# Placing the second half's gate operands and squares behind the gate's sigmoids

## The chip, the cores and the metric

One Trainium2 chip, one core of it. The metric is the device time of one execution in microseconds (us); of several executions the median is given. Engines are named as in the profile: PE is TensorE's matmul, PEld its weight load, DVE VectorE, ACT ScalarE, POOL GpSimd, SP SyncE (which issues most DMAs).

## What is computed

One layer of a decoder trunk for 1024 prompt positions and 8 single new tokens (1032 columns in all), model width 1024. After the mixing part and the squared-ReLU MLP, the layer ends with the step that matters here, and a final normalisation follows:

```
x = x + (p @ w_ple) * sigmoid(rms_norm(x, g_ple) @ w_ple_gate)     # p: (tokens, 256)
y = rms_norm(x, g_final)
```

Activations are kept transposed: the model width lies on partitions (8 blocks `m` of 128) and tokens lie along the free axis.

## The kernel before, in words

Each fp32 product is made of three fp32r products. An operand is split into a high part (`hi`, a cast on ACT) and a rest (`lo`, on DVE), and PE adds hi·hi, lo·hi and hi·lo.

**The two halves.** The down-projection of the MLP (`down`, L1434) and all that follows treat the tokens as two halves `nn` = 0, 1 of 516 columns. x lies in `ACC[:, ab, nn, p]` (L1309), where `m = p + 4*ab`. Half 0 is complete before the down stage ends, half 1 with its last steps.

**What the gate needs of x.** For each of the eight blocks (ab, p) of a half:
- `gate_in` (L1425) makes the matmul operands `XS[ab, nn]`: one ACT activation that scales by the gain `g_ple` (recorded as L166), and one DVE operation for the rest (L167). For half 1 these tiles are called `xt`, for half 0 `xs`.
- `add_ss` (L1389) adds the block's squares into `ss[:, nn]`: the first block by one ACT Square (L1398), each later one by an ACT Square into the only `sq` buffer (L1394) and a POOL add (L1395). It does so at high priority (`PRI`).

Then `rows_tok` (L1402) sums over partitions on PE (ten one-column matmuls into `ms`, L1408), takes the inverse root on DVE and puts it on diagonals in `sq`; `rows_all` (L1417) spreads it over all partitions (PE, `rB`, L1422) and two ACT copies (L1423) bring it back to `ss[:, nn]`, now the row factor `rr`. For half 0 `rows_all` is called in the last step of the down stage, so its two copies are the last readers of two of the down stage's eight PSUM banks.

**The gate stage.** From L1516 on, PSUM is four banks for gate sums (`psg2`, tile `g`) and four for all else (`pss2`, tag `s2`: the transposes `pT` of the embedding, the embedding products `em`, later the output's transposes `yT`). `gate_units` (L1639) walks over m and over two column blocks `n` of a half: 24 matmuls a unit (L1658 to L1660), then `evg` (L1642): DVE multiplies by `rr` (L1645), ACT takes the sigmoid (L1646), PE makes `em` (L1601 to L1603), DVE multiplies the two (L1647), POOL adds to x (L1649). The first sixteen units are half 0 (blocks 0 and 2), the other sixteen half 1 (blocks 1 and 3). The weights of a block m are cast two m ahead (`whi` on ACT, L150; `wlo` on DVE, L153). At the stage's start `w_ple` is loaded and split too (`wpl`, L1555 to L1559).

**The order.** On PE it is the order in which the code is traced, written out by hand: `weave` runs the gate units, each of which yields its cost in planned us, and wakes helpers at their due times (`spawn` and `wake`): `p_in` (L1566) makes the embedding's transposes, one every 0.5 planned us, ACT casting each (`pp`, L1582) and DVE taking the rest (L1583); `second_half` (L1680) issues one (ab, p) block of half 1 every 2.0 planned us from 6.0 on, and 4.0 after the last of these steps calls `rows(1)`; `first_out` makes the output of half 0. A gate result whose `rr` or embedding is not there yet is held back and evacuated when it `arrived` (L1671). On ACT, DVE and POOL the program's builder sets the order, from priorities and from its own estimate of when operands are ready; an engine then runs its instructions in that order. `tc.issue_after(ins)` places the instructions traced inside it behind `ins` on the engine of `ins`. `placed` (L1221) is a dictionary that the up stage already uses for such instructions.

Of the kernel before, what the change touches and what calls it, by code (L numbers as in the profile page):

```python
# [12 lines left out]
AF = mybir.ActivationFunctionType  # L13
ALU = mybir.AluOpType
# [13 lines left out]
PRI = 1000  # L28
# [56 lines left out]
def trunk_step_kernel(  # L85
# [35 lines left out]
    V, S, G, PE, SY = nc.vector, nc.scalar, nc.gpsimd, nc.tensor, nc.sync  # L121
# [23 lines left out]
    def f32(ap):  # L145
        return ap.bitcast(F32)
# [18 lines left out]
    def split_gain(dst, src, gain):  # L165
        S.activation(dst[0], src, AF.Copy, scale=gain)  # L166
        V.scalar_tensor_tensor(dst[1], in0=src, scalar=gain, in1=f32(dst[0]), op0=ALU.mult, op1=ALU.subtract)  # L167
# [52 lines left out]
    def spawn(gen, delay=0.0):  # L220
        tasks.append([clock[0] + delay, gen])
# [9 lines left out]
    def weave(main):  # L231


        for cost in main:
            clock[0] += cost
            wake()

    def drain(until=lambda: False):
        while tasks and not until():
            clock[0] = max(clock[0], min(t[0] for t in tasks))  # L240
            wake()
# [43 lines left out]
    with ExitStack() as mix:  # L285
# [46 lines left out]
        gmix, gff, gple, gfin = (vec[:, 8 * i : 8 * i + 8] for i in range(4))  # L332
# [21 lines left out]
        for n, (o, w) in enumerate(BLK):  # L354
# [20 lines left out]
            for k in range(KD):  # L375
# [6 lines left out]
                else:  # L382
# [3 lines left out]
                                       op0=ALU.mult, op1=ALU.mult)  # L386
# [834 lines left out]
    placed = {}  # L1221
# [87 lines left out]
    ACC = pacc.tile([P, 2, 2, 4, 516], F32, name="acc")  # L1309
# [13 lines left out]
    XS = {(ab, 0): [xst.tile([P, 4, 516], F32R, name=f"xs{ab}{i}") for i in range(2)] for ab in range(2)}  # L1323
# [62 lines left out]

    begun = set()

    def add_ss(ab, nn, p):  # L1389

        a = ACC[:, ab, nn, p]
        with tc.high_priority(PRI):
            if nn in begun:
                S.activation(sq, a, AF.Square)  # L1394
                G.tensor_add(ss[:, nn], ss[:, nn], sq)  # L1395
            else:
                begun.add(nn)
                S.activation(ss[:, nn], a, AF.Square)  # L1398
# [26 lines left out]
    def gate_in(ab, nn, p):  # L1425
        m = p + 4 * ab
        hi, lo = XS[ab, nn]
        split_gain((hi[:, p], lo[:, p]), ACC[:, ab, nn, p], gple[:, m : m + 1])
# [119 lines left out]
    def next_w():  # L1548

        halves()  # L1550
        stage()
        cur[0] += 1
        return ready[cur[0] - 1]
# [12 lines left out]
    def p_in():  # L1566

        for nn in range(2):
            for q0 in (0, 2, 4):
                qs = (q0, q0 + 1) if q0 < 4 else (4,)  # L1570
                if 4 in qs:
                    G.tensor_scalar_mul(pt8[nn], pt8[nn], mst[: TS // 2, nn, 4:5])
                for k in range(2):
                    ps = pss.tile([P, 512], F32, tag="s2", name="pT")
                    w = 0
                    for q in qs:
                        src = pt[:, pcol(nn, q), :] if q < 4 else pt8[nn]
                        r = rows_of(q)
                        PE.transpose(ps[:, w : w + r], src[:, k * P : (k + 1) * P], ident[:r, :r])
                        w += r  # L1580
                    hi, lo = (h[:, nn, q0 * P : q0 * P + w] for h in pp[k])
                    S.copy(hi, ps[:, :w])  # L1582
                    V.tensor_sub(lo, ps[:, :w], f32(hi))  # L1583
                    yield PT
            arrived("p", nn)

    def blk(v, n):

        return v[:, n % 2, TOFF[n // 2] : TOFF[n // 2] + WT[n // 2]]

    def x_of(m, n):
        return ACC[:, m // 4, n % 2, m % 4, TOFF[n // 2] : TOFF[n // 2] + WT[n // 2]]

    def emb(m, n):

        c = slice(m * P, m * P + P)
        ps = pss.tile([P, 512], F32, tag="s2", name="em")[:, : WT[n // 2]]
        for k in range(2):
            wh, wl = wpl[k]
            xh, xl = (blk(h, n) for h in pp[k])  # L1600
            PE.matmul(ps, lhsT=wh[:, c], rhs=xh, start=(k == 0), stop=False)  # L1601
            PE.matmul(ps, lhsT=wl[:, c], rhs=xh, start=False, stop=False)
            PE.matmul(ps, lhsT=wh[:, c], rhs=xl, start=False, stop=(k == 1))  # L1603
        return ps
# [5 lines left out]
    def rows(nn):  # L1610
        rows_tok(pss.tile([P, 512], F32, tag="s2", name="ms"), nn)
        yield 8.0
        rows_all(lambda: pss.tile([P, 512], F32, tag="s2", name="rB"), nn)
        arrived("r", nn)

    def y_out(nn, q):

        r = rows_of(q)
        c = pcol(nn, q)
        yo = ty.tile([P, D], F32, tag="yo", bufs=2, name="yo")  # L1620
        st = tp.tile([P, 2], F32, tag="st2", bufs=2, name="st2")
        pa = []
        for a in range(2):
            ps = pss.tile([P, 512], F32, tag="s2", name="yT")
            for j in range(4):
                PE.transpose(ps[:r, j * P : j * P + P], ACC[:, a, nn, j, q * P : q * P + r], ident)
            S.activation(yo[:r, :512], ps[:r], AF.Square, accum_out=st[:r, a : a + 1])
            pa.append(ps)
            yield YT
        V.tensor_add(st[:r, 0:1], st[:r, 0:1], st[:r, 1:2])  # L1630
        V.scalar_tensor_tensor(st[:r, 0:1], in0=st[:r, 0:1], scalar=1.0 / D, in1=ems[:r, nn, q : q + 1], op0=ALU.mult, op1=ALU.add)
        root(st[:r, 0:1], "ry", nn == 1)
        y = y_prompt[0, c * P : (c + 1) * P, :] if q < 4 else y_sample[4 * nn : 4 * nn + 4, 0, :]
        for a in range(2):
            b = slice(512 * a, 512 * a + 512)
            V.scalar_tensor_tensor(yo[:r, b], in0=pa[a][:r], scalar=st[:r, 0:1], in1=gfb[:r, b], op0=ALU.mult, op1=ALU.mult)
            SY.dma_start(y[:, b], yo[:r, b])

    def gate_units(blocks, last):  # L1639
        for m in range(KD):  # L1640

            def evg(ps, n, m=m):  # L1642
                w = WT[n // 2]
                t = tp.tile([P, 260], F32, tag="t", name="t")[:, :w]
                V.tensor_mul(t, ps, blk(rr, n))  # L1645
                S.activation(t, t, AF.Sigmoid)  # L1646
                V.tensor_mul(t, t, emb(m, n))  # L1647
                xv = x_of(m, n)
                (V if last and m > 5 else G).tensor_add(xv, xv, t)  # L1649

            ws = next_w()
            for n in blocks:
                w = WT[n // 2]
                ps = gps[0].tile([P, 512], F32, tag="g", name="g")[:, :w]
                for k in (4, 5, 6, 7, 0, 1, 2, 3):
                    wh, wl = (h[:, k % 4, :] for h in ws[k // 4])
                    xh, xl = (h[:, k % 4, TOFF[n // 2] : TOFF[n // 2] + w] for h in XS[k // 4, n % 2])
                    PE.matmul(ps, lhsT=wh, rhs=xh, start=(k == 4), stop=False)  # L1658
                    PE.matmul(ps, lhsT=wl, rhs=xh, start=False, stop=False)  # L1659
                    PE.matmul(ps, lhsT=wh, rhs=xl, start=False, stop=(k == 3))  # L1660
                    if k == 3:
                        with tc.high_priority(PRI):
                            if there >= {("p", n % 2), ("r", n % 2)}:
                                evg(ps, n)
                            else:
                                held.append((n, lambda ps=ps, n=n, evg=evg: evg(ps, n)))
                    yield 3 * w * 0.000455
# [12 lines left out]
    def second_half():  # L1680

        for p in range(4):
            for ab in (1, 0):
                gate_in(ab, 1, p)
                add_ss(ab, 1, p)
                yield 2.0
        yield 4.0
        yield from rows(1)

    def first_out():  # L1690
        for q in range(5):
            yield from y_out(0, q)

    with tc.manual_schedule(engines={mybir.EngineType.PE}):
        spawn(p_in())
        spawn(second_half(), 6.0)
        weave(gate_units((0, 2), False))
        spawn(first_out(), FIN0)
        weave(gate_units((1, 3), True))
        drain()  # L1700
        for q in range(5):
            for _ in y_out(1, q):
                pass
# [32 lines left out]
```

## Time and profile before

| | us |
|---|---|
| median of 3 runs (1418.0 to 1418.56) | 1418.04 |
| the profiled execution, its own time | 1419.37 |
| span of the profile, first to last instruction | 1417.7 |

Mean granted TensorE clock 0.965 of full speed. The end of the span is laid out like this: the down stage's last matmuls until 1254 us, the gate stage until 1396 us (half 1's units from 1327 us), and the output of half 1 until 1417.7 us. Busy time of an engine is shown with its share; an idle time in a row names what ended it in square brackets, behind an arrow.

### The profile page before, as it was taken

To read this page: it belongs to the slowest core of one execution; us is meant where nothing else is said; L and a number is where in the kernel's file an instruction comes from. 1 tells how busy PE (TensorE), PEld (TensorE's weight loads), DVE (VectorE), ACT (ScalarE), POOL (GpSimd) and SP (SyncE) were. 2 spreads that over 40 slices of the span, in tenths; PEclk is the share of its full clock that TensorE was granted. 3 is DMA by queue.
4 is the path that set the end of the run, shared out by engine and by line. 5 is a ranking of instruction groups with operands and counts; after the bars stand their busy time and mean duration, and the time that the engine had idled before them with its cause. 6 is when DMAs were issued, how large, how long until landed. Compare 5 with 4: busy or idle time off the path is not lost.

```text
span 1417.7 us, 26668 instructions
## 1 busy us (share of the span) xinstructions
PE 1314.5 (93%) x10189; PEld 1280.7 (90%) x10189; DVE 913.8 (64%) x1900; ACT 638.3 (45%) x1346; POOL 693.4 (49%) x720
## 2 busy tenths in 40 slices
PE   6979978999999799899999999789999999979995
PEld 5979968889899799899999999789999998979985
DVE  7745745465937757655544445677878787975564
ACT  6574645532233316556544555333433333552332
POOL 5300888857414405578848777731425156532110
PEclk9999988999999999999999999899999999999997
DMA  7234535555436721254446554873363523122221
GB/s 244 90 90 118 151 81 151 173 158 153 136 86 180 229 71 44 60 164 145 141 143 194 154 178 143 312 264 125 122 222 112 200 93 91 61 89 76 80 86 61
DMA packets 212076, 194.01 MB, mean 137 GB/s; under 512 B 20952, under 2 KB 181659, under 8 KB 211940
## 3 DMA queue, kind: packets, MB, share of 16 engines
q1 hardware_dynamic: 211436, 190.45, 43.5%
q8 instruction: 80, 1.31, 0.4%
q0 software_dynamic: 512, 1.85, 0.3%
q14 instruction: 48, 0.39, 0.1%
HBM read 131.75 MB, written 60.61 MB: 136 GB/s over the span
## 4 chain that ended last, share of the span: by engine, by line
PE 66%; DVE 11%; POOL 9%; ACT 4%; DMA 3%; issue 3%; SPq 0%; DVEq 0%; POOLq 0%; ACTq 0%
PE A L1184 9%; PE D L1184 6%; PE d L1457 6%; PE d L1458 6%; PE d L1456 6%; PE g L209 5%; PE g L211 5%; PE g L210 4%; PE C L1184 3%; PE B L1184 3%; POOL xinv L644 3%; POOL it L643 3%; DVE wlo L153 2%; PE g L1658 2%; PE g L1659 2%
## 5 line engine op out<-in xcount | busy, mean ns | idle before, releaser
L209 PE MATMUL g<-ra,whi 128*128 128x384 f32 (+3 forms) x800 | 273.2, 341 | 0.8 <-ACT ra L388 0.6
L1457 PE MATMUL d<-h,wlo 128*128 128x260 f32 (+1 forms) x896 | 256.9, 287 | 14.3 <-DVE wlo L153 14.3
L1456 PE MATMUL d<-h,whi 128*128 128x260 f32 (+1 forms) x896 | 254.6, 284 | 3.9 <-ACT whi L150 3.9
L211 PE MATMUL g<-ra,whi 128*128 128x384 f32 (+3 forms) x800 | 257.0, 321 | 0.8 <-POOL ra L389 0.4
L1458 PE MATMUL d<-h,whi 128*128 128x260 f32 (+1 forms) x896 | 256.1, 286 | 0.0
L210 PE MATMUL g<-ra,wlo 128*128 128x384 f32 (+3 forms) x800 | 255.9, 320 | 0.0
L1457 PEld LDWEIGHTS d<-h,wlo 128*128 128x128 f32 x896 | 171.4, 191 | 16.7 <-DVE wlo L153 16.7
L1456 PEld LDWEIGHTS d<-h,whi 128*128 128x128 f32 x896 | 172.1, 192 | 4.7 <-ACT whi L150 4.6
L1458 PEld LDWEIGHTS d<-h,whi 128*128 128x128 f32 x896 | 171.9, 192 | 0.0
L209 PEld LDWEIGHTS g<-ra,whi 128*128 128x128 f32 x800 | 154.9, 194 | 3.0 <-ACT ra L388 1.0
L211 PEld LDWEIGHTS g<-ra,whi 128*128 128x128 f32 x800 | 154.0, 193 | 2.5 <-POOL ra L389 1.6
L210 PEld LDWEIGHTS g<-ra,wlo 128*128 128x128 f32 x800 | 155.0, 194 | 0.7 <-DVE wlo L153 0.3
L153 DVE TENSOR_TENSOR wlo<-s,whi 128x512 fp32r<-128x512 f32 x96 | 73.7, 769 | 79.9 <-ACT whi L150 79.5
L153 DVE TENSOR_TENSOR wlo<-st,whi 128x512 fp32r<-128x512 f32 x94 | 72.3, 769 | 47.5 <-ACT whi L150 47.0
L1184 PE MATMUL A<-fb,whi 128*128 128x260 f32 (+1 forms) x512 | 95.6, 281 | 0.0
L643 POOL TENSOR_TENSOR it<-ainv,xinv 32x31 f32<-32x31 f32 (+15 forms) x124 | 74.5, 601 | 39.1 <-DMA ainv<-inv_d 29.7
L150 ACT CAST whi<-s 128x512 fp32r<-128x512 f32 x96 | 59.3, 618 | 73.8 <-PE D L1184 27.3
L1347 ACT CAST h<-raw 128x1024 fp32r<-128x1024 f32 (+1 forms) x56 | 58.7, 1055 | 68.3 <-DMA raw<-f_d 40.4
L150 ACT CAST whi<-st 128x512 fp32r<-128x512 f32 x96 | 59.0, 619 | 67.1 <-PE g L211 32.4
L1348 DVE TENSOR_TENSOR h<-raw,h 128x1024 fp32r<-128x1024 f32 (+1 forms) x56 | 76.8, 1380 | 14.6 <-ACT h L1347 14.5
L1465 DVE TENSOR_TENSOR acc<-acc,d 128x256 f32<-128x256 f32 (+1 forms) x192 | 75.0, 415 | 17.0 <-PE d L1458 16.1
L1214 ACT ACTIVATE q<-q 128x512 f32<-128x512 f32 (+1 forms) x124 | 75.9, 631 | 22.0 <-DVE q L1207 16.1
(433 smaller groups left out, 3532.2 us busy)
## 6 DMA issues: line engine op xcount, KB each, us to landing
a<-in_w_down SPq DMA_DIRECT2D x16, 1024.0 KB
raw<-f_d SPq DMA_DIRECT2D x28, 520.0 KB
raw<-f_d SPq DMA_DIRECT2D x28, 512.0 KB
st<-in_w_in SPq DMA_DIRECT2D x24, 512.0 KB
ck<-ck_d SPq DMA_DIRECT2D x32, 320.0 KB
ra<-in_w_up SPq DMA_DIRECT2D x32, 256.0 KB
rb<-in_w_up SPq DMA_DIRECT2D x32, 256.0 KB
st<-in_w_ple_gate SPq DMA_DIRECT2D x16, 512.0 KB
```

What stands on the lines that cost most here:

```text
L150: S.copy(dst_hi, src)
L153: lo_eng.tensor_sub(dst_lo, src, f32(dst_hi))
L209: PE.matmul(ps[:, :w], lhsT=whi[k], rhs=xh, start=(k == 0), stop=False)
L210: PE.matmul(ps[:, :w], lhsT=wlo[k], rhs=xh, start=False, stop=False)
L211: PE.matmul(ps[:, :w], lhsT=whi[k], rhs=xl, start=False, stop=(k == nk - 1))
L643: G.tensor_mul(tv, a, x)
L1184: PE.matmul(ps, lhsT=a[:, k, :], rhs=x[:, c, k, :], start=(first and k == 0 and j == 0), stop=(k == 3 and j == 2), skip_group_check=True)
L1214: placed["act"] = S.activation(v, v, func).ins
L1348: V.tensor_sub(lo[:, c], raw[:, c], f32(hi[:, c]))
L1456: PE.matmul(ps, lhsT=wh[:, k, :], rhs=xh[:, k, :], start=(k == 0), stop=False)
L1457: PE.matmul(ps, lhsT=wl[:, k, :], rhs=xh[:, k, :], start=False, stop=False)
L1458: PE.matmul(ps, lhsT=wh[:, k, :], rhs=xl[:, k, :], start=False, stop=(k == 3))
```

## The change

A sigmoid of the gate is remembered each time one is traced. `second_half` starts at 7.0 planned us and issues a block every 2.8. In it the ACT half of `gate_in` and the Square of `add_ss` are placed behind the latest sigmoid traced so far, the DVE half is written out beside them unplaced, and these squares have no raised priority. The step after the last block is 3.0.

```
-    def add_ss(ab, nn, p):
+    def add_ss(ab, nn, p, first=True):
         a = ACC[:, ab, nn, p]
-        with tc.high_priority(PRI):
+        with tc.high_priority(PRI if first else 0):
...
-                S.activation(t, t, AF.Sigmoid)
+                placed["sig"] = S.activation(t, t, AF.Sigmoid).ins
...
         for p in range(4):
             for ab in (1, 0):
-                gate_in(ab, 1, p)
-                add_ss(ab, 1, p)
-                yield 2.0
-        yield 4.0
+                m = p + 4 * ab
+                (hi, lo), x = XS[ab, 1], ACC[:, ab, 1, p]
+                with tc.issue_after(placed["sig"]):
+                    S.activation(hi[:, p], x, AF.Copy, scale=gple[:, m : m + 1])
+                V.scalar_tensor_tensor(lo[:, p], in0=x, scalar=gple[:, m : m + 1], in1=f32(hi[:, p]), op0=ALU.mult, op1=ALU.subtract)
+                with tc.issue_after(placed["sig"]):
+                    add_ss(ab, 1, p, False)
+                yield 2.8
+        yield 3.0
         yield from rows(1)
...
-        spawn(second_half(), 6.0)
+        spawn(second_half(), 7.0)
```

## Rows read from the trace of the kernel before

**Rows 1.** The profile's page, part 1: busy time, share of the span and instructions of each engine.
```profile
PE 1314.5 (93%) x10189; PEld 1280.7 (90%) x10189; DVE 913.8 (64%) x1900; ACT 638.3 (45%) x1346; POOL 693.4 (49%) x720
```

**Rows 2.** The view of waits, PE alone, from 1250 us to the end: who waited, for what, us in total, times, longest.
```profile
PE yT L1626 <- DVE yo L1636: 7.6, 4, 4.2
PE pT L1579 <- ACT ss L1423: 7.1, 1, 7.1
PE em L1601 <- DVE yo L1636: 2.4, 1, 2.4
PE pT L1579 <- DVE t L1647: 1.2, 1, 1.2
```

**Rows 3.** The chain that ended last, in order of time, from 1247 to 1280 us: start us, us, what.
```profile
1248.78 7.61 DMA st<-in_w_ple
1256.40 1.04 ACT wpl L150
```

**Rows 4.** The timeline of ACT: start us, us, line, operation, tiles, shapes, count.
```profile
1257.36 3.19 ACT L166 ACTIVATE xt<-acc,vec 128x516 fp32r<-128x516 f32 x5
1260.44 0.35 ACT L1423 COPY ss<-rB 128x256 f32<-128x256 f32 x1
1260.70 1.96 ACT L166 ACTIVATE xt<-acc,vec 128x516 fp32r<-128x516 f32 x3
1262.55 0.36 ACT L1423 COPY ss<-rB 128x260 f32<-128x260 f32 x1
...
1265.21 0.63 ACT L1394 ACTIVATE sq<-acc 128x516 f32<-128x516 f32 x1 [1.15 <-POOL ss L1395]
...
1270.26 1.28 ACT L1646 ACT_TABLE_LOAD   x1
1271.55 0.42 ACT L1646 ACTIVATE t<-t 128x256 f32<-128x256 f32 x1
...
1272.46 0.61 ACT L150 CAST whi<-st 128x512 fp32r<-128x512 f32 x1
...
1279.19 0.42 ACT L1646 ACTIVATE t<-t 128x256 f32<-128x256 f32 x1 [0.85 <-DVE t L1645]
...
1286.38 0.42 ACT L1646 ACTIVATE t<-t 128x256 f32<-128x256 f32 x1 [3.12 <-DVE t L1645]
```

**Rows 5.** The timeline of PE around the start of the gate stage, with the two steps of `rows(1)` at its end.
```profile
1253.49 1.03 PE L1422 MATMUL rB<-sq,ones 128*128 128x256 f32 x4
...
1255.54 0.28 PE L1660 MATMUL g<-xs,whi 128*128 128x256 f32 x1
1262.97 0.69 PE L1579 MATMUL pT<-ident,pt 128*128 128x128 f32 x2 [7.14 <-ACT ss L1423]
...
1266.17 0.38 PE L1579 MATMUL pT<-ident,pt 128*128 128x128 f32 x2
...
1267.11 0.38 PE L1579 MATMUL pT<-ident,pt 128*128 128x128 f32 x2
...
1270.17 0.28 PE L1601 MATMUL em<-pp,wpl 128*128 128x256 f32 x1
...
1273.35 0.28 PE L1660 MATMUL g<-xs,whi 128*128 128x256 f32 x1
1274.85 0.44 PE L1579 MATMUL pT<-ident,pt 128*128 128x128 f32 x2 [1.22 <-DVE t L1647]
...
1302.78 1.07 PE L1408 MATMUL ms<-ones,ss 128*128 128x1 f32 x10
...
1314.22 1.03 PE L1422 MATMUL rB<-sq,ones 128*128 128x256 f32 x4
```

**Rows 6.** Half-microsecond stretches of PE: from:to, length, busy us (instructions), granted clock (1.00 is 2.4 GHz, 0.50 is 1.2 GHz), DMA share, GB/s.
```profile
1259.00:1259.50 0.50, 0.00 (x0) 0.50 0.12 35
...
1265.50:1266.00 0.50, 0.50 (x5) 0.68 0.00 0
...
1361.50:1362.00 0.50, 0.50 (x4) 0.50 0.99 361
...
1364.50:1365.00 0.50, 0.50 (x5) 0.69 0.00 0
```

**Rows 7.** The timeline of PE after a shorter wait, in half 1; the second and the third row are the first and the last of 16 matmuls in a row.
```profile
1360.44 0.36 PE L1601 MATMUL em<-pp,wpl 128*128 128x256 f32 x1 [2.35 <-DVE yo L1636]
...
1361.49 0.42 PE L1660 MATMUL g<-xt,whi 128*128 128x260 f32 x1
...
1364.74 0.32 PE L1660 MATMUL g<-xt,whi 128*128 128x260 f32 x1
```

**Rows 8.** The timeline of DVE at the start of the gate stage.
```profile
1258.62 5.42 DVE L167 SCALAR_TENSOR_TENSOR xt<-acc,vec,xt 128x516 fp32r<-128x516 f32 x8
...
1273.10 1.37 DVE L153 TENSOR_TENSOR wlo<-st,whi 128x512 fp32r<-128x512 f32 x1 [0.88 <-ACT whi L150]
1274.39 0.41 DVE L1647 TENSOR_TENSOR t<-t,em 128x256 f32<-128x256 f32 x1
...
1281.53 0.69 DVE L153 TENSOR_TENSOR wlo<-st,whi 128x512 fp32r<-128x512 f32 x1 [1.46 <-ACT whi L150]
```

**Rows 9.** The timeline of POOL at the same place.
```profile
1272.63 1.28 POOL L1395 TENSOR_TENSOR ss<-ss,sq 128x516 f32<-128x516 f32 x1 [1.34 <-ACT sq L1394]
```

**Rows 10.** Busy time in one long stretch of half 0's units: from:to, length, PE, PEld, DVE, ACT, POOL (instructions), clock, DMA share, GB/s.
```profile
1276.50:1336.00 59.50, 59.50 (x497) 59.04 (x496) 28.69 (x71) 18.38 (x40) 13.43 (x18) 1.00 0.25 72
```

## The prediction

> **What bounds the kernel now.** I read the page's part 1 first: PE is busy for 93% of the span [rows 1], so other engines' work costs time only where PE stands still or runs at the lower clock. Next comes the view of waits for PE, from the start of the gate stage on [rows 2]: of its 18.3 us, 10.0 belong to the output stage (yT and em behind yo), which the change does not touch; 7.1 are one single wait for the copy `ss` (L1423), 1.2 another for `t` (L1647). These two lie where the change is made.
>
> The chain says what came before the copy [rows 3]: the DMA of `w_ple` lands at 1256.40, and ACT casts it until 1257.44. The ACT timeline shows the rest [rows 4]: five of half 1's `xt` activations run ahead of the first copy and three more ahead of the second, which ends at 1262.91. The factors `rB` that are copied were finished by PE at 1254.52 [rows 5]. PE's first transpose `pT` needs the PSUM bank that the second copy gives back, so PE stands from 1255.82 to 1262.97. Nobody needs `xt` before half 1's units, some 65 us later; ACT runs them because their operands are there. After the wait PE runs at 1.2 GHz: the granted clock is 0.50 from 1259.0 and rises at about 1265.7 [rows 6]. Two groups of two transposes and six matmuls took 1263.0 to 1266.17, 3.20 us, and the next group at full clock 0.94 [rows 5], so the clock costs 3.20 - 1.88 = 1.32 us.
>
> The second wait (1.22 us at 1274.85) [rows 5]: a `pT` needs the `s2` bank that held the first `em`; that is free when DVE has done t·em, 1274.39 to 1274.80, and this stood behind a `wlo` of 1.37 us [rows 8], whose cast ran at 1272.46 behind a Square that came late [rows 4].
>
> From 1276.5 to 1336.0 PE is never idle [rows 10], so what is won before that is carried through half 0.
>
> **The change, part by part.**
>
> *The eight `xt` activations leave the place ahead of the copies.* They are now behind a sigmoid, and the first sigmoid needs transposes that wait for the copies; so no `xt` can be ahead of them. The copies then follow the last `wpl` cast: first at about 1257.36 (where the first `xt` started), second 0.26 us later, the pitch from a copy to the next instruction [rows 4], ending at 1257.62 + 0.36 = 1257.98. PE resumes 0.06 us later as before, at 1258.04 instead of 1262.97: **-4.93 us**. Bounds: not less, unless other ACT work takes the place (a rival); at most 2.2 more, the remaining wait from 1255.82, if the copies also got ahead of the `wpl` casts. I take the low end: the builder had five `xt` between `wpl` and the copies, so by its own estimate the copies were ready later than the casts, and nothing in the change makes them ready sooner.
>
> *The clock.* A wait of 2.2 us remains. The trace has one of 2.35 us at 1360.44; behind it the clock fell too, and 16 matmuls from 1361.49 to 1364.74 came 0.217 us apart [rows 6, 7], against 59.50/497 = 0.120 [rows 10]: 15 × 0.097 = 1.45 us. The ends are 0 (clock kept, gain 1.32) and 1.45. I take 1.45, the nearest wait in length: **+0.13 us**.
>
> *The squares leave the embedding's casts alone.* Before, each Square waited about 1.15 us for the POOL add that frees `sq` [rows 4], with the `pp` casts queued behind it on ACT. Now the first sigmoid comes right behind the casts and its table load (1.28 us), and t·em of the first unit can run once `em` is done, before the `pT` that waited. If DVE keeps its order, with `wlo` ahead, t·em waits for the weights' cast, which PE releases at the end of the second unit, 1272.4 before and so no later relative to PE; with `wlo` at 0.69 instead of 1.37 [rows 8] and its cast not behind a Square (0.1), the wait shrinks from 1.22 to about 0.45. Ends: 0 and 1.22; I take the unchanged order: **-0.8 us**.
>
> *What the gate stage takes on.* ACT gets eight times 0.72 + 0.64 us, DVE eight L167 (5.42 us in all) [rows 8], POOL eight adds of 1.28 [rows 9]. A block falls due every 2.8 planned us. Two sigmoids of the same column block, two units apart, stand 7.19 us apart [rows 4], against 24 × 516 × 0.000455 = 5.63 planned: one planned us is 1.28 real, so a block comes about every 3.6 us, one a unit. Per unit ACT then holds 0.42 + 0.62 + 1.36 = 2.4 of 3.6 us, and DVE and POOL were busy for 48% and 23% of the stretch [rows 10]. Queued behind a placed pair are the next sigmoid and weight cast. A sigmoid late by 1.4 us holds one of four gate banks longer, a cast is needed two units after its buffer is free: nothing on PE, **0**. Without that cover (the pressed banks of the first three units) it could cost up to one pair, 1.36.
>
> *`rows(1)` moves* from 6.0 + 16.0 + 4.0 = 26.0 to 7.0 + 22.4 + 3.0 = 32.4 planned us, its spread from 34.0 to 40.4; each wake is rounded up to the next gate step, some 2 us more in all. Half 1's first unit begins at 8 × 5.63 = 45.1, so the spread is still ahead of it. DVE has 8 planned us, here 1314.22 - 1302.78 = 11.4 real [rows 5], as before. The eighth block starts at the earliest 5.8 planned (7.4 real) us ahead of the sums, and takes about 4.2: gate multiply and sigmoid 0.85, `xt` 0.72, Square 0.64, perhaps an x add 0.74, its own add 1.28. Slack 3.2 us: **0**. The first Square, issued early in the down stage, goes with them; ACT waited there anyway: 0. No DMA is added or moved; the gate weights' loads follow PE's releases and come earlier with them.
>
> **Sum:** -4.93 + 0.13 - 0.8 = -5.6 us. The profiled execution took 1419.37 (its span 1417.7 and 1.67 around it), 1.33 above the median; it would come to 1413.8, the median to 1418.04 - 5.6 = **1412.4 us**.
>
> **The rivals.**
>
> 1. *All of the wait goes.* The copies run at 1254.6, the clock stays, the second wait goes: 2.2 + 4.93 + 1.32 + 1.22 = 9.7, so 1408.4. Against it: the order just argued. Chance 0.12.
> 2. *Collisions in the first units.* A `wlo` that ran beside an add of squares took 1.37 us, one with POOL idle 0.69 [rows 8, 9]. The adds, once bunched in 16 us, are now spread over eight units, and each holds DVE up to its 1.28 us. On PE's path is only what the `s2` banks wait for while `p_in` still runs: two such, 2.6 us, leaving 3.0: 1415.0. Against: DVE is idle half the time, and the first placed pair comes after the second sigmoid. Chance 0.12. The Trainium skill has the rule ("SBUF — State Buffer", Who interferes with whom): a VectorE instruction with two SBUF inputs and a GpSimd one that reads SBUF share a read port, and the second waits until the first has finished. By that rule, the trace's 1.37 us agrees, and it speaks against spreading the adds.
> 3. *It doesn't do it.* Other work takes the place of `xt` ahead of the copies, or what PE wins is lost at the output stage, whose order the builder also sets anew: 1417 to 1419. For it: 10.0 us of PE's waits stand there. Against: they are DVE's own chain, which shifts with PE. Chance 0.11.
> 4. *Slower.* The blocks slip: one `sq` buffer ties each Square to the add before it, and POOL runs that add behind an x add that waits for t·em. If each block slips 1.5 us past its unit, the eighth is 12 late; PE stands at the sums for what goes beyond the 3.2 slack, 8.8 us: +3.2, so 1421.2. It decides from 3.2 us of slip in all, and is slower than before from 8.8. Against: 2.4 of 3.6 us on ACT. Chance 0.07.
>
> **How the numbers follow.** The forecast has 0.58; its own range, from a clock that stays and no second wait (-7.5) to no gain from the second wait (-4.8), is 1410.5 to 1413.2. The range reaches to rivals 1 and 2: 1408.3 to 1415.2, leaving out rivals 3 and 4. A measurement of this kernel tells about 0.2%, 2.8 us, from no change: forecast and rivals 1 and 2 are faster (0.82), rival 3 the same (0.11), rival 4 slower (0.07).
>
> **What would show it.** On ACT the two copies stand right behind the `wpl` casts and all `xt` behind sigmoids, one a unit; PE's wait for L1423 is 2.2 us, its clock falls once, the wait for L1647 is under 0.5 us, and no wait stands at L1408 or L1422. I am wrong if the copies are still late, if PE waits for `ss` of half 1 or for `pp`, or if the second half of the stage grows by what the first loses.

## The result, and the profile after

The changed kernel takes 1412.03 us (median of 19 runs, 1407.09 to 1418.24), the kernel before 1418.32 beside it (19 runs, 1415.17 to 1424.89). The two medians are 6.3 us apart; the ratio on record, which is not that of the medians, is 0.9946, interval 0.9935 to 0.9957: 7.7 us less (6.1 to 9.2). The forecast was 1412.4, 5.6 us less than before.

The profiled execution of the changed kernel is its longest: 1418.24 us. It reached the gate stage 9.2 us later than the profiled execution of before did, by differences ahead of the changed code (the same kernel reached it at 1253.49 in e8, below), so the two spans (1416.5 and 1417.7) are not compared. What is compared is one stretch, called the stage from here on: from the start of its first rB matmul (L1422) to the start of the first output transpose yT (L1626). Before, it lasts from 1253.49 [rows 5] to 1333.6, 80.1 us; after, from 1262.70 to 1334.0, 71.3 us. The second profile of the changed kernel, e8, gives 72.0. So the stage is shorter by 8.1 to 8.8 us, which the interval of the whole runs holds.

The page of the changed kernel, part 1, answers to [rows 1]. The share of PE is the same 93%; a gain of half a per cent can't be read there.

```profile
PE 1317.7 (93%) x10189; PEld 1286.1 (91%) x10189; DVE 920.8 (65%) x1900; ACT 639.4 (45%) x1346; POOL 696.9 (49%) x720
```

The view of waits of PE from 1250 us to the end (who waited, for what, us in total, times, longest) answers to [rows 2]: the 7.1 for `ss` has become 1.6, the 1.2 for `t` is gone, and of the output stage's two waits behind `yo` one is 7.9 instead of 7.6 and the other 2.4 as before.

```profile
PE yT L1626 <- DVE yo L1636: 7.9, 4, 4.2
PE em L1601 <- DVE yo L1636: 2.4, 1, 2.4
PE pT L1579 <- ACT ss L1423: 1.6, 1, 1.6
```

The timeline of ACT answers to [rows 4]:

```profile
1263.43 1.99 ACT L150 CAST wpl<-st 128x1024 fp32r<-128x1024 f32 x2
1265.32 0.64 ACT L1423 COPY ss<-rB 128x256 f32<-128x256 f32 x2
...
1270.34 1.28 ACT L1646 ACT_TABLE_LOAD   x1
1271.64 0.42 ACT L1646 ACTIVATE t<-t 128x256 f32<-128x256 f32 x1
...
1274.92 0.42 ACT L1646 ACTIVATE t<-t 128x260 f32<-128x260 f32 x1
1275.24 0.71 ACT L1687 ACTIVATE xt<-acc,vec 128x516 fp32r<-128x516 f32 x1
1275.86 0.62 ACT L1398 ACTIVATE ss<-acc 128x516 f32<-128x516 f32 x1
...
1279.54 0.42 ACT L1646 ACTIVATE t<-t 128x256 f32<-128x256 f32 x1 [0.84 <-DVE t L1645]
1279.87 0.71 ACT L1687 ACTIVATE xt<-acc,vec 128x516 fp32r<-128x516 f32 x1
1280.48 0.62 ACT L1394 ACTIVATE sq<-acc 128x516 f32<-128x516 f32 x1
```

The two copies run right behind the casts of `w_ple`, 0.26 us apart (0.64 us for both). Every `xt` now follows a sigmoid, with its Square behind it. The timeline of PE answers to [rows 5]:

```profile
1262.70 1.03 PE L1422 MATMUL rB<-sq,ones 128*128 128x256 f32 x4
...
1266.01 0.44 PE L1579 MATMUL pT<-ident,pt 128*128 128x128 f32 x2 [1.60 <-ACT ss L1423]
...
1267.01 0.38 PE L1579 MATMUL pT<-ident,pt 128*128 128x128 f32 x2
...
1271.96 0.28 PE L1601 MATMUL em<-pp,wpl 128*128 128x256 f32 x1
...
1275.26 0.38 PE L1579 MATMUL pT<-ident,pt 128*128 128x128 f32 x2
...
1309.89 1.07 PE L1408 MATMUL ms<-ones,ss 128*128 128x1 f32 x10
```

The first group of transposes, with its six matmuls, takes 1.00 us (1266.01 to 1267.01), where before the first two groups together took 3.20 us [rows 5]; and the `pT` that waited 1.22 us, here at 1275.26, has no wait any more. The view of busy time in stretches (columns as in [rows 10]) shows the granted clock behind the wait at 1.00, where before it was 0.50 [rows 6], and half 0's units with PE never idle, as before [rows 10], while DVE's share has risen from 28.69 of 59.5 to 37.81 of 57.5 us:

```profile
1266.00:1267.00 1.00, 0.99 (x8) 0.99 (x9) 0.97 (x2) 0.37 (x1) 1.00 (x1) 1.00 1.20 310
...
1276.50:1334.00 57.50, 57.50 (x480) 57.04 (x480) 37.81 (x75) 24.92 (x50) 23.95 (x23) 1.00 0.25 74
```

### The profile page after: what moved, and what is told of

Read it like the earlier page. It is cut to its first block, busy times and chain, and to the rows that moved or that the text cites. A ratio compares the mean times of both kernels' runs of the same rounds, so it can differ in the third digit from the quotient of the medians.

```text
span 1416.5 us, 26668 instructions
## 1 busy us (share of the span) xinstructions
PE 1317.7 (93%) x10189; PEld 1286.1 (91%) x10189; DVE 920.8 (65%) x1900; ACT 639.4 (45%) x1346; POOL 696.9 (49%) x720
## 4 chain that ended last, share of the span: by engine, by line
PE 72%; DVE 9%; POOL 7%; ACT 4%; DMA 3%; issue 3%; SPq 1%; DVEq 0%; ACTq 0%; POOLq 0%
PE A L1184 9%; PE d L1457 7%; PE d L1458 7%; PE d L1456 7%; PE D L1184 7%; PE g L209 5%; PE g L211 5%; PE g L210 5%; PE B L1184 3%; PE C L1184 3%; PE g L1658 2%; POOL it L643 2%; POOL xinv L644 2%; PE g L1660 2%; PE g L1659 2%
## 5 line engine op out<-in xcount | busy, mean ns | idle before, releaser
L209 PEld LDWEIGHTS g<-ra,whi 128*128 128x128 f32 x800 | 156.6, 196 | 3.0 <-ACT ra L388 1.0
L211 PEld LDWEIGHTS g<-ra,whi 128*128 128x128 f32 x800 | 155.8, 195 | 2.5 <-POOL ra L389 1.7
L153 DVE TENSOR_TENSOR wlo<-s,whi 128x512 fp32r<-128x512 f32 x96 | 73.5, 768 | 81.7 <-ACT whi L150 81.4
L153 DVE TENSOR_TENSOR wlo<-st,whi 128x512 fp32r<-128x512 f32 x94 | 75.8, 807 | 40.8 <-ACT whi L150 40.1
L150 ACT CAST whi<-st 128x512 fp32r<-128x512 f32 x96 | 59.1, 619 | 60.8 <-PE g L211 31.6
L644 POOL TENSOR_TENSOR xinv<-xinv,it 32x31 f32<-32x31 f32 (+15 forms) x124 | 79.0, 637 | 9.6
```

The costliest lines, as they stand in the source:

```text
L150: S.copy(dst_hi, src)
L153: lo_eng.tensor_sub(dst_lo, src, f32(dst_hi))
L209: PE.matmul(ps[:, :w], lhsT=whi[k], rhs=xh, start=(k == 0), stop=False)
L211: PE.matmul(ps[:, :w], lhsT=whi[k], rhs=xl, start=False, stop=(k == nk - 1))
L644: G.tensor_sub(X[:, j + 1 :, :w], X[:, j + 1 :, :w], tv)
```

## The experiments

The theory: the eight `xt` activations ahead of the copies held PE, and taking them away is most of the gain. The rivals: the squares' new place gives it, or the later due times do. Each run's profile gives the parts of the stage from the timeline of PE, in us: from the first rB to the first pT, to the first em, to the first yT; their sum; then the part from yT to the start of the last L1658 (the gate's last unit), in which the change places nothing.

| kernel | wait for L1423 | rB to pT | pT to em | em to yT | stage | yT to last L1658 |
|---|---|---|---|---|---|---|
| before | 7.14 | 9.5 | 7.2 | 63.4 | 80.1 | 60.2 |
| changed | 1.60 | 3.3 | 6.0 | 62.0 | 71.3 | 58.7 |
| changed again (e8) | 1.75 | 4.1 | 5.9 | 62.0 | 72.0 | 59.1 |
| e1 operands only | 1.35 | 3.6 | 7.2 | 63.4 | 74.3 | 60.4 |
| e2 squares only | 6.51 | 8.8 | 7.5 | 62.0 | 78.4 | 57.0 |
| e3 due times only | 7.16 | 9.0 | 8.6 | 62.2 | 79.8 | 60.6 |
| e4 copies first | none | 2.1 | 5.9 | 62.0 | 70.0 | 60.6 |
| e9 copies first again | none | 2.2 | 5.9 | 62.0 | 70.1 | 60.5 |
| e5 two ahead | 2.47 | 4.8 | 7.5 | 62.0 | 74.3 | 60.5 |
| e6 four ahead | 4.21 | 6.5 | 8.6 | 62.0 | 77.1 | 60.5 |
| e7 sums early | 1.78 | 4.1 | 6.0 | 67.1 | 77.2 | 57.0 |

**e1: the gate operands placed, the squares not.** In the changed kernel:

```
-                with tc.issue_after(placed["sig"]):
-                    add_ss(ab, 1, p, False)
+                add_ss(ab, 1, p)
```

> The changed kernel with the squares put back as before (high priority, not placed); only the xt activations stay behind the sigmoids, and the due times stay changed. Theory (the copies' place on ACT is most of it): PE's wait for L1423 is 1.6 to 2.3 us instead of 7.1, the squares queue the embedding's casts behind POOL adds again, so a wait for L1647 of 0.4 to 1.2 us may come back; from the sums' spread of half 0 (first L1422) to the first output transpose (first L1626) 71.5 to 73.5 us, against 80.1 before and 71.3 changed; 5 to 8 us faster than before. Rival (the squares are the cause): the long wait stays, at most 1.5 us faster.

Measured: 1413.93 us (9 runs), ratio 0.9958 (0.9941 to 0.9976); stage 74.3 (71.5 to 73.5 was expected), so 5.9 of the 8.1 to 8.8 us come with the `xt` alone. The timeline of ACT shows the copies at the front and what stands behind them instead, a Square that waits for POOL, with the cast `pp` queued behind it; the waits of PE show what that costs, and the timeline of DVE the first t·em:

```profile
1256.88 0.64 ACT L1423 COPY ss<-rB 128x256 f32<-128x256 f32 x2
...
1261.35 0.64 ACT L1394 ACTIVATE sq<-acc 128x516 f32<-128x516 f32 x1 [2.92 <-POOL ss L1395]
1261.89 0.35 ACT L1582 CAST pp<-pT 128x256 fp32r<-128x256 f32 x1
```

```profile
PE em L1601 <- DVE pp L1583: 1.7, 2, 0.9
PE pT L1579 <- ACT ss L1423: 1.4, 1, 1.4
```

```profile
1268.97 0.41 DVE L1647 TENSOR_TENSOR t<-t,em 128x256 f32<-128x256 f32 x1
```

The granted clock is 1.00 throughout here, and still PE needs as long from the first pT to yT as before: 70.6 us, where the changed kernel needs 67.9 to 68.0. With the Squares in their old place the first t·em ends 11.8 us after the first pT, at the full clock of e1 (1257.58 to 1269.38) as behind the low one of before (1262.97 to 1274.80 [rows 5, 8]); in the changed kernel it ends 7.6 to 7.7 us after it. So behind the wait it is the queue of Squares, POOL adds and `pp` casts that sets PE's pace, and a clock that stays high gains nothing while this queue is there.

**e2: the squares placed, the operands not.** In the changed kernel:

```
-                with tc.issue_after(placed["sig"]):
-                    S.activation(hi[:, p], x, AF.Copy, scale=gple[:, m : m + 1])
+                S.activation(hi[:, p], x, AF.Copy, scale=gple[:, m : m + 1])
```

> The changed kernel with the xt activations not placed; only the squares stay behind the sigmoids. Theory: the wait for L1423 stays near 7 us with the low clock behind it, and only the wait for L1647 (1.2 us) goes; first L1422 to first L1626 78.5 to 80 us; 0 to 1.5 us faster than before. Rival (the squares are the cause): 5 us faster or more.

Measured: 1418.17 us (12 runs), ratio 0.9993 (0.9973 to 1.0013), no difference that can be told; stage 78.4, 1.7 shorter. From the first pT to yT it is 1.1 us shorter (69.6), with the first t·em ending 9.3 us after the first pT. The timeline of PE keeps the long wait:

```profile
1264.16 0.69 PE L1579 MATMUL pT<-ident,pt 128*128 128x128 f32 x2 [6.51 <-ACT ss L1423]
```

**e3: the due times alone.** In the kernel before:

```
-                yield 2.0
-        yield 4.0
+                yield 2.8
+        yield 3.0
...
-        spawn(second_half(), 6.0)
+        spawn(second_half(), 7.0)
```

> The kernel before with only the due times changed (start 7.0, a block every 2.8, 3.0 behind the last). Theory: the due times order only what is traced, ACT runs xt and squares as early as before, so nothing changes: waits of 7.1 and 1.2 us as before, first L1422 to first L1626 80 us, within 1.5 us of before. Rival (the spreading in time is what frees ACT): 4 us faster or more.

Measured: 1420.07 us (12 runs), ratio 0.9997 (0.9979 to 1.0015); stage 79.8. The timeline of ACT has the five `xt` ahead of the first copy as before [rows 4], and PE waits 7.16. Due times that are later do not hold back an activation whose operands are there.

```profile
1263.91 3.19 ACT L166 ACTIVATE xt<-acc,vec 128x516 fp32r<-128x516 f32 x5
1267.01 0.35 ACT L1423 COPY ss<-rB 128x256 f32<-128x256 f32 x1
```

One thing came out otherwise than expected: the 1.22 us wait for `t` [rows 5] was gone here too, with the squares where they had been. It was not won, though. The clock stayed low longer (0.50 until after 1275, 8.6 instead of 7.2 us from pT to em), so PE came later to the `pT` that had waited; the first t·em ended 12.0 us after the first pT, no earlier than before, and from pT to yT the stage took 70.8 us, as before (70.6).

**e4 and e9: the copies ahead of the weights' casts.** The changed kernel, the casts of `w_ple` placed behind the last copy; e9 is e4 once more, beside e8, which is the changed kernel as it is:

```
-                S.copy(ss[:, nn, c], ps)
+                placed["ss"] = S.copy(ss[:, nn, c], ps).ins
...
-        split(wpl[k][0][:, :], wpl[k][1][:, :], st[:, :], S, V)
+        with tc.issue_after(placed["ss"]):
+            split(wpl[k][0][:, :], wpl[k][1][:, :], st[:, :], S, V)
```

> The changed kernel with the two casts of w_ple also placed, behind the second copy of half 0's factors. Theory: what is left of the wait for L1423 is the copies standing behind these casts, so it falls from 1.6 to 0.1 to 0.4 us, the clock stays at full speed, em does not wait for wpl (needed 6 us later); first L1422 to first L1626 69.5 to 70.5 us; 1 to 2 us faster than the changed kernel, 8 to 10 faster than before. Rival: the casts then hold the embedding's casts and PE waits for pp or for a bank instead, no gain over the changed kernel.

> The changed kernel itself once more, for a second profile and beside the next run. Expected: wait for L1423 of 1.4 to 2.3 us, whatever the earlier stages' times; first L1422 to first L1626 71 to 73 us (73 if the clock falls behind the wait); 0.9935 to 0.996 of before.

> The changed kernel with the casts of w_ple behind the copies, once more and beside the changed kernel on the same chip. Theory: wait for L1423 gone, first L1422 to first L1626 70 us, 1 to 2 us faster than the changed kernel. Rival: no difference that shows in whole runs.

Measured: e4 1412.56 us (6 runs), ratio 0.9942 (0.9922 to 0.9963); e9 1412.76 (6 runs), 0.9931 (0.9911 to 0.9952); e8 1414.39 (8 runs), 0.9951 (0.9927 to 0.9974). The stage of both is 70.0 to 70.1, against 71.3 and 72.0 of the changed kernel, and the wait for L1423, expected at 0.1 to 0.4 us in e4, is gone. The timelines of ACT and of PE in e4:

```profile
1258.66 0.72 ACT L1423 COPY ss<-rB 128x256 f32<-128x256 f32 x2
1259.27 2.01 ACT L150 CAST wpl<-st 128x1024 fp32r<-128x1024 f32 x2
```

```profile
1257.93 1.03 PE L1422 MATMUL rB<-sq,ones 128*128 128x256 f32 x4
...
1260.07 0.38 PE L1580 MATMUL pT<-ident,pt 128*128 128x128 f32 x2
```

The copies end at 1259.38, and the transposes follow without a wait. In the stage this is 1.2 to 2.0 us better than the changed kernel; in whole runs the intervals overlap, so there the 1 to 2 us that were expected are not established.

**e5 and e6: two or four `xt` let ahead.** The changed kernel, the first two activations not placed (in e6 the first four, with `>= 4`):

```
-                with tc.issue_after(placed["sig"]):
+                with tc.issue_after(placed["sig"]) if 2 * p + 1 - ab >= 2 else ExitStack():
                     S.activation(hi[:, p], x, AF.Copy, scale=gple[:, m : m + 1])
```

> The changed kernel with the first two xt activations not placed, so that two of them stand ahead of the two copies on ACT again. Theory (PE waits for the copies, and each activation ahead of them costs its pitch of 0.62 us, from five in 3.09 us before): PE's wait for L1423 is 1.5 + 1.24 = 2.7 us (2.4 to 3.1); the clock falls behind it, so first L1422 to first L1626 grows by 1.2 to 2.8 over the changed kernel's 71.3, to 72.5 to 74. Rival (the wait depends on something else, a DMA or the squares): the wait stays at 1.6.

> The changed kernel with the first four xt activations not placed, four of them ahead of the copies on ACT. Theory: wait for L1423 of 1.5 + 2.48 = 4.0 us (3.6 to 4.4), low clock behind it, first L1422 to first L1626 75 to 77 us. Rival: the wait stays at 1.6.

Measured, one execution each (1418.73 and 1417.39 us; their place in whole runs isn't told by one): the waits are 2.47 and 4.21 us, as expected, and the stages 74.3 and 77.1, just above what was expected. ACT and PE in e5, then in e6:

```profile
1260.25 1.05 ACT L150 CAST wpl<-st 128x1024 fp32r<-128x1024 f32 x1 [0.16 <-DMA st<-in_w_ple]
1261.20 1.34 ACT L1687 ACTIVATE xt<-acc,vec 128x516 fp32r<-128x516 f32 x2
1262.45 0.62 ACT L1423 COPY ss<-rB 128x256 f32<-128x256 f32 x2
```

```profile
1263.12 0.44 PE L1579 MATMUL pT<-ident,pt 128*128 128x128 f32 x2 [2.47 <-ACT ss L1423]
```

```profile
1256.65 1.04 ACT L150 CAST wpl<-st 128x1024 fp32r<-128x1024 f32 x1 [0.26 <-DMA st<-in_w_ple]
1257.60 2.57 ACT L1687 ACTIVATE xt<-acc,vec 128x516 fp32r<-128x516 f32 x4
1260.08 0.62 ACT L1423 COPY ss<-rB 128x256 f32<-128x256 f32 x2
```

```profile
1260.75 0.69 PE L1579 MATMUL pT<-ident,pt 128*128 128x128 f32 x2 [4.21 <-ACT ss L1423]
```

With 0, 2, 4 and 8 `xt` ahead, PE waits 1.60 to 1.75, 2.47, 4.21 and 7.14 us. These waits also depend on how late the casts of `w_ple` end, which differs from execution to execution. From the end of the last cast to the first pT it is 0.6, 1.8, 3.1 and 5.5 us (1265.42 to 1266.01 in the changed kernel, 1261.30 to 1263.12, 1257.69 to 1260.75, 1257.44 to 1262.97 before): 0.61 us for each activation, which is the time from the start of one to the start of the next (four in 2.48 us in e6, 0.62). The place of these activations is the cause of the wait.

**e7: the sums early.** The changed kernel, with half 1's sums (L1408) due as soon as the last block is issued, to measure how much slack the blocks leave:

```
-                yield 2.8
-        yield 3.0
+                if (ab, p) != (0, 3):
+                    yield 2.8
         yield from rows(1)
```

> The changed kernel with the sums of half 1 (ms) issued right behind the eighth block instead of 5.8 planned us later; on PE they stand 72 matmuls earlier, 8.6 us at 0.12 each. Theory (the due times leave slack, 5.5 us from the end of the last add of squares to ms in the changed kernel's trace): PE waits for the add of squares at L1408, 8.6 - 5.5 = 3.1 us (2.4 to 3.8), perhaps with a low clock behind it; first L1422 to first L1626 73.5 to 76.5 against 71.3. Rival (the blocks finish long before, the due times matter for nothing): no wait at L1408.

Measured: PE waits 1.84 us at the sums for the last add, less than the 2.4 to 3.8 expected, since the expectation counted 72 matmuls between the old place and the new; by the traces it was 63 (306 instead of 369 from the first rB on), 7.3 us. The timelines of POOL and PE:

```profile
1299.31 1.73 POOL L1395 TENSOR_TENSOR ss<-ss,sq 128x516 f32<-128x516 f32 x1
```

```profile
1301.09 1.39 PE L1408 MATMUL ms<-ones,ss 128*128 128x1 f32 x10 [1.84 <-POOL ss L1395]
```

The granted clock then fell, as the stretches of PE show, and the stage, 77.2, is 5.2 us longer than in e8 and longer than expected (73.5 to 76.5): a wait of 1.84 that cost nearly three times its length.

```profile
1302.00:1303.00 1.00, 1.00 (x6) 0.95 (x7) 0.41 (x4) 0.00 (x0) 0.00 (x0) 0.50 0.00 0
...
1308.00:1309.00 1.00, 1.00 (x8) 1.00 (x8) 0.84 (x5) 0.00 (x0) 0.03 (x1) 0.70 0.69 195
```

## Why the prediction was right, and which terms were off

The mechanism was the one forecast, and the time, 1412.03 against 1412.4, is inside the range. That it is only 0.4 us off is partly luck: the gain, 7.7 us by the ratio and 8.1 in the stage, is over 2 us more than the 5.6 forecast, and the price behind the wait was wrong. By its own steps, with e8's execution as the measure of the changed kernel, since there the small wait of L1658 behind `acc` (0.7 us) is present as before:

- **The `xt` away from the copies: forecast -4.93, measured -5.4** (rB to pT, 9.5 to 4.1). The copies follow the casts and PE waits 1.60 or 1.75 us, where 2.2 were forecast. The forecast kept the casts' place in time of before; they ended 3.95 us after the start of rB then [rows 3, 5]; they end 3.46 us after it in e8, and that is the 0.5 us by which the term was short. It is not the change's, since in e2 and e3, where the `xt` stand ahead, they end 3.30 and 3.44 us after it. From the last cast to the first pT the change takes 5.53 to 0.60, the 4.93 of the forecast. The low end that was taken, copies behind the casts, was the right one; the 2.2 us held out for copies ahead of them are real too, as 1.60 to 1.75 (e4, e9).
- **The clock and the second wait: forecast +0.13 and -0.8, measured -2.7 together** (from pT to yT, 70.6 to 67.9). These are the terms that were mis-sized. The clock stayed at 1.00 behind 1.60 and 1.75 us, where the nearest wait in length, 2.35 us, had been followed by the low clock [rows 7]; the second wait went from 1.22 us to none. By the table it looks like -1.3 for the clock (pT to em) and -1.4 for the wait (em to yT), but e1 shows that the two cannot be priced apart: its clock stayed too, and its 70.6 us are those of before. The squares' place alone, at the low clock, gives 1.1 us (e2), the kept clock alone none (e1), both 2.7. The forecast had named the queue, `pp` casts behind Squares that wait for POOL, but priced only the 1.22 us of PE's wait that it left at the low clock, and not the 4 us by which it held back the first t·em.
- **Why no second wait was left.** The order of DVE was the one assumed, `wlo` ahead of t·em. But the cast of that `wlo` does not wait for the end of the second unit, as the forecast had it: in the changed kernel it ran at 1272.00, 2.07 us ahead of that unit's last matmul, and t·em ended at 1273.68, 1.58 us before the `pT` at 1275.26. The timelines of ACT, PE and DVE:

```profile
1272.00 0.62 ACT L150 CAST whi<-st 128x512 fp32r<-128x512 f32 x1
```

```profile
1274.07 0.28 PE L1660 MATMUL g<-xs,whi 128*128 128x260 f32 x1
```

```profile
1272.66 0.69 DVE L153 TENSOR_TENSOR wlo<-st,whi 128x512 fp32r<-128x512 f32 x1 [0.36 <-ACT whi L150]
1273.27 0.41 DVE L1647 TENSOR_TENSOR t<-t,em 128x256 f32<-128x256 f32 x1
```

- **Together** the forecast's own other ends, -4.93 - 1.32 - 1.22 = -7.5, come near the -8.1 in the stage and the -7.7 in whole runs.
- **The gate stage's new load: forecast 0, measured 0.** Between 1276.5 and 1334.0 PE is busy for 57.50 of 57.50 us, and from em to yT the changed kernel takes no longer than e3, which has no activation placed there (62.0 and 62.2).
- **The moved sums: forecast 0 with 3.2 us of slack, measured 0 with 5.5.** The last add starts at 1302.63 and ends at 1304.38; the sums start at 1309.89 without a wait. e7 agrees: moved 7.3 us ahead, they should wait 7.3 - 5.5 = 1.8 us, and waited 1.84.

**Rival 1** (all of the wait goes, -9.7) is what e4 and e9 make of the kernel: -10.1 in the stage of both. It needs the copies ahead of the casts, which the change alone doesn't bring. **Rival 3** fell with the trace's order and with the output stage's waits, which hardly moved. **Rival 4** needed the blocks to slip; they came one a unit.

**Rival 2**, the collisions, did take place. The timelines of DVE and of POOL in the changed kernel:

```profile
1280.61 1.17 DVE L1688 SCALAR_TENSOR_TENSOR xt<-acc,vec,xt 128x516 fp32r<-128x516 f32 x1 [0.20 <-ACT xt L1687]
...
1281.92 1.57 DVE L153 TENSOR_TENSOR wlo<-st,whi 128x512 fp32r<-128x512 f32 x1
...
1283.75 0.68 DVE L153 TENSOR_TENSOR wlo<-st,whi 128x512 fp32r<-128x512 f32 x1
```

```profile
1280.49 0.74 POOL L1649 TENSOR_TENSOR acc<-acc,t 128x256 f32<-128x256 f32 x1 [3.14 <-DVE t L1647]
1281.19 1.75 POOL L1395 TENSOR_TENSOR ss<-ss,sq 128x516 f32<-128x516 f32 x1
...
1302.63 1.75 POOL L1395 TENSOR_TENSOR ss<-ss,sq 128x516 f32<-128x516 f32 x1
```

A `wlo` and an operand's second half that meet a POOL add take 1.57 and 1.17 us; the `wlo` that meets none takes 0.68, and an `xt` that starts ahead of the POOL add beside it (1276.00) 0.75. The one that started later is the one that gets longer, in a row here: the `xt` behind the add to x (L1649), the add of squares behind the `xt`, the `wlo` behind the add of squares. Both DVE instructions end about 0.55 us after the add that was ahead of them (1281.78 after 1281.23, 1283.49 after 1282.94), and so did the `wlo` of before (1274.47 after 1273.91 [rows 8, 9]). The add of squares takes 1.75 behind an `xt`; ahead of a `wlo` it took 1.28 [rows 9]. The Trainium skill ("SBUF — State Buffer", Who interferes with whom) has two such instructions compete for one read port, and the trace agrees. It costs PE nothing: it is busy for all of the 57.50 us, while DVE has 20 of them left. What decides is not that two engines collide but whether anyone waits for the later one.

## What to carry to other kernels

When the bounding engine waits for a short copy, look at what the copying engine does just ahead of it: work whose operands are early and whose result nobody needs for 65 us can stand in front of it, at its full time from start to start (here 0.61 us each). Place such work behind an instruction that lies past the wait; a later due time alone did not move it (e3). And price a wait with what it does to the clock behind it, with both ends, but look first whether something else sets the pace there: a clock that stayed high was worth nothing until the Squares had left the queue (e1), and some 1.6 us once they had (e2 against the changed kernel, from pT to yT).

## What the runs showed of the hardware that was not expected

The granted clock behind a wait of PE does not follow from the wait's length alone. At the start of the gate stage it stayed at 2.4 GHz behind 1.35 us (e1), 1.60, 1.75 and 1.78 (e7), and fell to 1.2 GHz behind 2.47 (e5), 4.21 and 6.51 to 7.16; behind 1.84 at the sums (e7) it fell. In the output stage the same `em` waits for `yo` in every kernel: behind 2.35 (before) and 2.61, 2.64, 2.71, 2.71, 2.73 and 2.80 us (e6, e9, e4, e5, e3, e1) it fell, behind 2.37 (changed) and 2.81 (e8) it stayed. The wait and the stretch behind it in e8:

```profile
1352.77 0.35 PE L1601 MATMUL em<-pp,wpl 128*128 128x256 f32 x1 [2.81 <-DVE yo L1636]
```

```profile
1354.00:1356.00 2.00, 2.00 (x19) 2.00 (x18) 1.81 (x8) 0.74 (x2) 0.73 (x1) 1.00 0.44 166
```

Where it stayed, the part from yT to the last L1658 took 58.7 and 59.1 us, where it fell 60.2 to 60.6; in e2 and e7, where that wait was 0.7, it stayed and the part took 57.0. The change places nothing there, and the changed kernel and the one before wait alike (2.37 and 2.35), so 1.5 us of a single profile's difference can come from the clock alone. What tells the waits behind which it fell from those behind which it stayed is open, and so is why two of the kernels wait only 0.7.
